# An MLP up projection by seven block products, and a down projection 512 columns at a time

## The chip, the cores and the metric

The kernel runs on one core of one Trainium2 chip. The metric is the device time of one execution in microseconds; a kernel's time is the median of its runs.

## What is computed

One layer of a bidirectional encoder, batch 1, 512 tokens, width 1024, f32. A modulation vector comes from c; then

```python
h = rmsnorm(x, norm_mix_w[l]) * (1.0 + scale1) + shift1
proj = h @ w_in[l]
y_ssd = ssd_mixer(z, xbc, dt_raw, ...)      # Mamba-2 SSD, 16 heads, both directions
y_hg = hgrn2_mixer(q, f_fwd, f_bwd, i, g, ...)  # HGRN2, 8 heads, both directions
y = jnp.concatenate([y_ssd, y_hg], axis=-1).astype(x.dtype) @ w_out[l]
x = x + gate1 * y
h = rmsnorm(x, norm_mlp_w[l]) * (1.0 + scale2) + shift2
x = x + gate2 * (jnp.square(jax.nn.relu(h @ w_up[l])) @ w_down[l])
```

and a last RMSNorm. `w_up` is 1024 x 4096, `w_down` 4096 x 1024. The MLP takes 512 tokens through both.

## The kernel before

All large products are made in three parts. An f32 operand is split into `hi`, its value rounded to the type fp32r that TensorE reads in one pass, and the residue `lo`; a product is hi·hi + hi·lo + lo·hi, three matmuls into one PSUM tile. The split of a piece of 128 x 512 weights is a cast on ScalarE (`hi`) and a subtraction on VectorE (`lo`). Raw weights come by DMA from SyncE's queue into four buffers (`raw`), split pieces lie in seven (`hi`, `lo`).

TensorE's instructions keep the order of the code. Those of the other engines are put in order by the compiler's scheduler, under the buffers and the data they wait for. In the mixing stage the code itself decides when a side stream (the SSD, the HGRN2 heads, the modulation sums) issues its next step: `Clock` adds up estimated costs, and `tick()` advances a stream that is due while the estimate of VectorE's and ScalarE's work is less than 3.5 us ahead of TensorE's.

PSUM has eight buffers of 128 x 512 in four rings: `mm` 2, `sc` 3, `tr` 2, `y` 1.

After the output projection (x in `x1`, tokens on partitions) the MLP begins. `h2_tile(tt)` turns the normalised rows of one tile of 128 tokens into columns: eight transposes, scale and shift out of PSUM (half on VectorE, half on ScalarE), then the split into `g_hi` and `g_lo`, whose partitions are the width and whose columns are the tokens. In the code tiles 0 and 1 stand within the output projection, tiles 2 and 3 among the first up products.

The MLP goes through four blocks of 1024 hidden columns. A block has four up units and four down units. An up unit takes 256 hidden columns: for each of two column tiles, eight row tiles of the width, three matmuls of 512 tokens each (`mm_T`); `relu2` takes the result out of PSUM (relu, square, split into `uh` and `ul`, two passes on each of ScalarE and VectorE). A down unit takes 256 output columns: for each of the four token tiles, eight hidden tiles, three matmuls of 256 columns (`mm_N`), and `gated_add` multiplies by the gate and adds to `x1`, both on VectorE. The pieces of the next unit are loaded and split while a unit runs. The first unit and a half run in halves of 256 tokens, so that they can begin before tiles 2 and 3 of h exist. In the last unit each token tile is normalised and stored as it ends.

In the SSD, `intra(q)` multiplies, for each of four heads, a 128 x 128 matrix `es` with 64 columns of `xs`, in f32, into the PSUM tile `py`. There are two groups, four chunks, eight heads in each.

Of the kernel before, what the change touches and what calls it, by code (L numbers as in the profile page):

```python
# [151 lines left out]
def encoder_layer(  # L152
# [1208 lines left out]
    first = unit_split(mload(units[0]))
    raw2 = mload(units[1])
    w = unit_split(raw2, range(3))
    os_ = [psum("mm"), psum("mm"), psum("sc")]
    for j in range(2):
        mm_T(first, j, g_hi, g_lo, pst=os_[j], n=256)
        h2_tile(2 + j)
    mm_T(w, 0, g_hi, g_lo, pst=os_[2], n=256, ks=range(6))
    for j in range(2):
        mm_T(first, j, g_hi, g_lo, pst=os_[j], n0=256, n=256)  # L1370
        relu2(units[0], j, os_[j])
    w += unit_split(raw2, range(3, 4))
    mm_T(w, 0, g_hi, g_lo, pst=os_[2], n=256, ks=range(6, 8))
    mm_T(w, 0, g_hi, g_lo, pst=os_[2], n0=256, n=256)
    units = units[1:]
    for i, u in enumerate(units):
        nw = []
        if i + 1 < len(units):
            nxt = mload(units[i + 1])
            nw = unit_split(nxt, range(3))  # L1380

        def last():
            if nw:
                nw.extend(unit_split(nxt, range(3, 4)))
        if u[0] == "up":
            for j in range(2):
                if j:
                    pend.append(last)
                relu2(u, j, os_[2] if i == j == 0 else mm_T(w, j, g_hi, g_lo, hook=tick))
        else:  # L1390
            while len(gate2) <= u[2] // 2:
                bga.advance()

            def lh(k, tt, fb_=u[1]):
                return us[fb_, k][0][:, tt * P:(tt + 1) * P]

            def ll(k, tt, fb_=u[1]):
                return us[fb_, k][1][:, tt * P:(tt + 1) * P]
            if u == units[-1]:
                fnw = mp.tile([P, D], F32, tag="fnw", name="fnw")  # L1400
                nc.scalar.dma_start(out=fnw, in_=final_norm_w.partition_broadcast(P))
                c = slice(768, 1024)
                for tt in range(NT):
                    row_head(tt, 768)
                    V.tensor_tensor(out=xn2[:, tt, :768], in0=x1[:, tt, :768], in1=fnw[:, :768], op=MULT)
                for tt in range(NT):
                    o = psum("mm")
                    mm_N(w, tt, lh, ll, o[:, :256], 256)
                    gated_add(o[:, :256], tt, 1, c, gate2)
                    row_rstd(tt, 768)  # L1410
                    r = rs2[:, tt:tt + 1]
                    n = 448 if tt == 3 else 768
                    A.activation(xn2[:, tt, :n], xn2[:, tt, :n], AF.Copy, scale=r)
                    V.scalar_tensor_tensor(out=xn2[:, tt, c], in0=x1[:, tt, c], scalar=r, in1=fnw[:, c], op0=MULT, op1=MULT)
                    if n < 768:
                        V.tensor_scalar(out=xn2[:, tt, n:768], in0=xn2[:, tt, n:768], scalar1=r, scalar2=None, op0=MULT)
                        nc.scalar.dma_start(out=out2d[tt * P:(tt + 1) * P, :n], in_=xn2[:, tt, :n])
                        nc.sync.dma_start(out=out2d[tt * P:(tt + 1) * P, n:], in_=xn2[:, tt, n:])
                    else:
                        nc.sync.dma_start(out=out2d[tt * P:(tt + 1) * P, :], in_=xn2[:, tt, :])  # L1420
                break
            if u[2] == 0:

                os_ = [psum("mm"), psum("mm"), psum("sc"), psum("sc")]
                for k0, k1 in ((0, 6), (6, 8)):
                    for tt in range(NT):
                        mm_N(w, tt, lh, ll, os_[tt][:, :256], 256, ks=range(k0, k1))
                    if k0 == 0:
                        last()
                for tt in range(NT):  # L1430
                    gated_add(os_[tt][:, :256], tt, 1, slice(0, 256), gate2)
            for pair in range(2 if u[2] else 0):
                o = psum("mm")
                for i2 in range(2):
                    if pair and i2:
                        pend.append(last)
                    mm_N(w, 2 * pair + i2, lh, ll, o[:, i2 * 256:(i2 + 1) * 256], 256, hook=tick)
                gated_add(o, 2 * pair, 2, slice(u[2] * 256, u[2] * 256 + 256), gate2)
        w = nw


# [32 lines left out]
```

## Time and profile before

| | us |
|---|---|
| median of three runs | 995.55 (994.33 to 995.98) |
| profiled execution, its own time | 997.37 |
| its span, first to last instruction | 995.6 |

The profile is one execution. TensorE (PE) is the busiest engine; PEld is its weight load, which overlaps matmuls; DVE is VectorE, ACT is ScalarE. Operations are recorded by helpers, so lines 106, 170 and 175 stand for nearly all of them: groups are told apart by the names of their tiles. `ps_mm<-hi,uh` is a matmul into `mm`. One f32 matmul (not fp32r) shows as two records.

### The profile page before, as it was taken

Reading aid. Unit: us, or ns where it says so; the run is one execution under the profiler, and the core shown is the slowest. Engines: PE = TensorE matmul, PEld = TensorE weight load, DVE = VectorE, ACT = ScalarE, POOL = GpSimd, SP = SyncE. Lnnn points to the kernel's source line nnn. Section 1 sums busy time; section 2 is a strip of 40 time slices with the busy share of each in tenths; the row PEclk is TensorE's granted clock in tenths of the full one; section 3 lists DMA queues with packets and bytes.
Section 4 is the critical chain, followed back from the end, with each engine's and each line's share of the span. In section 5 each row is a group of like instructions: output and inputs, shape, how many; then the busy total and the mean of one; then the engine's idle time right before and its main releaser. Section 6 shows DMA issues by size and latency. Waiting matters only on the chain.

```text
span 995.6 us, 17588 instructions
## 1 busy us (share of the span) xinstructions
PE 962.5 (97%) x6886; PEld 843.9 (85%) x6886; DVE 649.2 (65%) x1189; ACT 493.9 (50%) x965; POOL 48.1 (5%) x91
## 2 busy tenths in 40 slices
PE   5999999999999999989999999999999999999997
PEld 4788887788877888879998899979988998998897
DVE  4478869887989475877777677665544455444445
ACT  6367647857675366565555225642233234214414
POOL 0000000010000000000111211000000000000000
PEclk9999999999999989999999999999999999999999
DMA  9953422334422333222656875133332233223322
GB/s 272 266 134 82 111 76 64 86 96 127 109 81 77 97 106 84 66 75 65 191 168 191 283 244 147 58 114 100 98 114 85 86 105 106 88 85 96 105 66 85
DMA packets 114791, 116.70 MB, mean 117 GB/s; under 512 B 8556, under 2 KB 103445, under 8 KB 114709
## 3 DMA queue, kind: packets, MB, share of 16 engines
q1 hardware_dynamic: 106213, 86.45, 29.7%
q0 software_dynamic: 8064, 28.32, 9.2%
q8 instruction: 54, 0.88, 0.4%
q10 hardware_dynamic: 432, 0.82, 0.2%
q14 instruction: 28, 0.23, 0.1%
HBM read 113.39 MB, written 2.16 MB: 116 GB/s over the span
## 4 chain that ended last, share of the span: by engine, by line
PE 87%; DVE 4%; DMA 3%; ACT 3%; issue 2%; SPq 0%; DVEq 0%; ACTq 0%; POOLq 0%
PE ps_mm L170 65%; PE ps_sc L170 13%; PE ps_tr L170 4%; PE ps_y L170 3%; PE ps_tr L175 2%; DMA raw<-in_w_in_dram 1%; DMA e<-cdr 1%; DVE K L106 1%; ACT hi L106 1%; DMA adaw<-in_ada_w_dram 1%; ACT t L106 1%; DVE lo L106 0%; DVE ada L106 0%; DVE Q L106 0%; DVE t L106 0%
## 5 line engine op out<-in xcount | busy, mean ns | idle before, releaser
L106 ACT CAST hi<-raw 128x512 fp32r<-128x512 f32 (+1 forms) x276 | 167.1, 614 | 240.7 <-PE ps_mm L170 156.7
L106 DVE TENSOR_TENSOR lo<-raw,hi 128x512 fp32r<-128x512 f32 (+1 forms) x276 | 185.5, 681 | 108.4 <-ACT hi L106 106.2
L170 PE MATMUL ps_mm<-hi,uh 128*128 128x256 f32 x448 | 125.8, 281 | 0.0
L170 PE MATMUL ps_mm<-hi,ul 128*128 128x256 f32 x448 | 125.4, 280 | 0.0
L170 PE MATMUL ps_mm<-lo,uh 128*128 128x256 f32 x448 | 125.4, 280 | 0.0
L170 PE MATMUL ps_mm<-hi,h_hi 128*128 128x256 f32 (+1 forms) x384 | 114.3, 298 | 0.0
L170 PE MATMUL ps_mm<-h_hi,hi 128*128 128x512 f32 x256 | 107.9, 422 | 1.1 <-ACT h_hi L106 1.1
L170 PE MATMUL ps_mm<-lo,h_hi 128*128 128x256 f32 (+1 forms) x384 | 108.2, 282 | 0.0
L170 PE MATMUL ps_mm<-hi,h_lo 128*128 128x256 f32 (+1 forms) x384 | 108.1, 282 | 0.0
L170 PE MATMUL ps_mm<-h_hi,lo 128*128 128x512 f32 x256 | 101.7, 397 | 0.0
L170 PE MATMUL ps_mm<-h_lo,hi 128*128 128x512 f32 x256 | 101.5, 397 | 0.0
L170 PE MATMUL ps_mm<-m_hi,hi 128*128 128x512 f32 (+1 forms) x264 | 100.7, 381 | 0.7 <-ACT m_hi L106 0.7
L170 PE MATMUL ps_mm<-m_lo,hi 128*128 128x512 f32 (+1 forms) x264 | 100.7, 382 | 0.6 <-DVE m_lo L106 0.6
L170 PE MATMUL ps_mm<-m_hi,lo 128*128 128x512 f32 (+1 forms) x264 | 100.7, 382 | 0.0
L170 PEld LDWEIGHTS ps_mm<-hi,uh 128*128 128x128 f32 x448 | 84.3, 188 | 0.4 <-issue 0.2
L170 PEld LDWEIGHTS ps_mm<-lo,uh 128*128 128x128 f32 x448 | 84.2, 188 | 0.4 <-issue 0.2
L170 PEld LDWEIGHTS ps_mm<-hi,ul 128*128 128x128 f32 x448 | 84.4, 188 | 0.0
L106 ACT ACTIVATE t<-ps_mm 128x512 f32<-128x512 f32 x63 | 37.4, 594 | 76.8 <-PE ps_mm L170 76.2
L170 PEld LDWEIGHTS ps_mm<-hi,h_hi 128*128 128x128 f32 x384 | 72.4, 189 | 3.5 <-issue 1.7
L170 PEld LDWEIGHTS ps_mm<-lo,h_hi 128*128 128x128 f32 x384 | 72.5, 189 | 1.9 <-issue 1.7
L170 PEld LDWEIGHTS ps_mm<-hi,h_lo 128*128 128x128 f32 x384 | 72.4, 189 | 0.0
L106 DVE TENSOR_TENSOR t<-t 128x512 f32<-128x512 f32 x32 | 22.1, 692 | 64.9 <-ACT uh L106 64.9
(301 smaller groups left out, 1967.6 us busy)
## 6 DMA issues: line engine op xcount, KB each, us to landing
raw<-in_w_in_dram SPq DMA_DIRECT2D x68, 256.0 KB, 2.9
adaw<-in_ada_w_dram POOLq DMA_DIRECT2D x32, 512.0 KB, 5.1
raw<-in_w_up_dram SPq DMA_DIRECT2D x64, 256.0 KB, 3.0
raw<-in_w_down_dram SPq DMA_DIRECT2D x64, 256.0 KB, 3.1
raw<-in_w_in_dram SPq DMA_DIRECT2D x104, 128.0 KB, 2.8
ada_in<-in_ada_w_dram SPq DMA_DIRECT2D x16, 512.0 KB, 6.1
e<-cdr POOLq DMA_DIRECT2D x32, 256.0 KB, 3.6
raw<-in_w_out_dram SPq DMA_DIRECT2D x32, 256.0 KB, 5.1
```

The costliest lines, as they stand in the source:

```text
L106: return f(*args, **kw)
L170: return tc.keep_in_program_order(nc.tensor.matmul(**kw))
L175: return tc.keep_in_program_order(nc.tensor.transpose(**kw))
```

## The change

The up projection. The 1024 x 512 matrix of h (width by tokens) is cut into 2 x 2 blocks, A11 (width 0 to 511, tokens 0 to 255), A12 (width 512 to 1023), A21 and A22 (tokens 256 to 511), and a group of hidden columns of `w_up` likewise into B11, B12, B21, B22 (512 rows by 256 columns, the two column halves 512 apart). Instead of eight block products there are seven (Winograd's form), on sums of blocks:

| product | h | weights |
|---|---|---|
| P1 | A11 | B11 |
| P2 | A12 | B21 |
| Q3 | S4 = A12 - S2 | B22 |
| Q4 | A22 | last sum of weights |
| Q5 | S1 = A21 - A22 | B11 + B12 |
| Q6 | S2 = A11 - S1 | B11 + B12 + B22 |
| Q7 | S3 = A11 - A21 | B12 + B22 |

(the signs are folded into the combinations). `h_sums` makes the four sums of h once, on VectorE, and splits them. For each of the eight groups (four blocks, two groups each) `up_prep` makes four sums of weight blocks on VectorE, each 128 x 1024, and splits fourteen pieces; the first two groups take the pieces of P1 and P2 from the row loads. A product is 2 column tiles x 4 row tiles x 3 matmuls of 256 columns. Its result is combined with earlier ones by VectorE on the way out of PSUM; `relu2` then works on 1024 elements at once, with three passes on ScalarE and one on VectorE. `ahead()` keeps seven split pieces in front of the one in use.

The down projection. `dn_wide` takes 512 output columns, the hidden tile in the outer loop and four token tiles in four PSUM tiles. In the last block columns 512 to 1023 keep 256 columns at a time (`dn_narrow`).

The start. `h2_tile` leaves its rows in `xn2`, from which `h_sums` reads. P1 and P2 of both first groups run before the rest, around `h2_tile(2)` and `h2_tile(3)`.

The SSD. Each product of `intra` becomes two, of 64 output rows each.

```diff
             def intra(q):
                 for h in range(4):
                     c0_ = (4 * q + h) * 64
-                    PE.matmul(out=py[:, c0_:c0_ + 64], lhsT=es[cc, q][:, h, :], rhs=yv[:, c0_:c0_ + 64], start=True, stop=True)
+                    for t0 in (0, 64):
+                        PE.matmul(out=py[t0:t0 + 64, c0_:c0_ + 64], lhsT=es[cc, q][:, h, t0:t0 + 64], rhs=yv[:, c0_:c0_ + 64],
+                                  start=True, stop=True)
...
     def h2_tile(tt):
         for q in range(2):
             pt = psum("tr")
-            hraw = tmp()[:, :T]
+            hraw = xn2[:, tt, q * T:(q + 1) * T]
...
+            if q == 0 and tt >= 2:
+                continue
             hv = hraw.rearrange("p (j n) -> p j n", n=P)
...
+    def h_sums():
...
+        V.tensor_tensor(out=fold(s1), in0=A21, in1=A22, op=SUB)
+        V.tensor_tensor(out=fold(s2), in0=A11, in1=fold(s1), op=SUB)
+        V.tensor_tensor(out=fold(s3), in0=A11, in1=A21, op=SUB)
+        V.tensor_tensor(out=fold(s4), in0=A12, in1=fold(s2), op=SUB)
...
+        for name, v, hi, lo in zip(("S2", "S1", "S3", "S4"), (s2, s1, s3, s4), his, los):
+            A.copy(out=hi, in_=v)
+            V.tensor_tensor(out=lo, in0=v, in1=hi.bitcast(F32), op=SUB)
...
+    def up_load(g, b):
...
+        t = up_.tile([P, 4, 256], F32, tag="xr", name=nm("xr"), bufs=5)
+        r, c0_ = (b // 10 - 1) * 512, g // NS * 1024 + (b % 10 - 1) * 512 + g % NS * 256
+        nc.sync.dma_start(out=t, in_=w_up2[r:r + 512, c0_:c0_ + 256].rearrange("(k p) n -> p k n", p=P))
+        blocks_in[g, b] = t
+
+    def up_prep(g):
+        early = g < NS
...
+        if not early:
+            yield from halves(b11)
+        V.tensor_tensor(out=b11, in0=b11, in1=b12, op=ADD)
+        x2 = up_.tile([P, 4, 256], F32, tag="xr", name=nm("xr"), bufs=5)
+        V.tensor_tensor(out=x2, in0=b11, in1=b22, op=ADD)
+        yield from halves(x2)
+        yield from halves(b11)
+        up_load(g + 1, 11)
+        V.tensor_tensor(out=b12, in0=b12, in1=b22, op=ADD)
+        yield from halves(b12)
+        up_load(g + 1, 12)
+        if not early:
+            yield from halves(b21)
+        yield from halves(b22)
+        up_load(g + 1, 22)
+        V.tensor_tensor(out=x2, in0=x2, in1=b21, op=ADD)
+        yield from halves(x2)
+        up_load(g + 1, 21)
...
+    def up_step(g, what, tag):
+        o = psum(tag)
+        for i in range(2):
+            hi, lo = pieces[used[0]]
+            for k in range(4):
+                mh_, ml_ = mov[PRODUCTS[what]](k)
+                mm3(o[:, i * 256:(i + 1) * 256], hi[:, k, :], lo[:, k, :], mh_, ml_, k == 0, k == 3)
+            used[0] += 1
+            ahead()
...
+        if what == "Q6":
+            wt_[g] = tmp()[:, :T].rearrange("p (i n) -> p i n", n=256)
+            V.tensor_tensor(out=wt_[g], in0=o3, in1=p1s[g], op=SUB)
+        elif what == "Q5":
+            tt_[g] = tmp()[:, :T].rearrange("p (i n) -> p i n", n=256)
+            V.tensor_tensor(out=tt_[g], in0=o3, in1=wt_[g], op=ADD)
+        elif what == "Q7":
+            V.tensor_tensor(out=c22, in0=tt_[g], in1=o3, op=SUB)
+            V.tensor_tensor(out=c21, in0=o3, in1=wt_[g], op=SUB)
...
+    def relu2(g, half):
+        r = rt[g][half]
...
+        A.activation(r, r, AF.Relu)
+        A.activation(r, r, AF.Square)
+        A.copy(out=uh, in_=r)
         V.tensor_tensor(out=ul, in0=r, in1=uh.bitcast(F32), op=SUB)
...
+    def dn_wide(fb_, c, tags):
+
+        os_ = [psum(t) for t in tags]
+        for n_, k in enumerate(KDN):
+            hi, lo = pieces[used[0]]
+            for tt in range(NT):
+                uh, ul = u_at(fb_, k, tt)
+                PE.matmul(out=os_[tt], lhsT=uh, rhs=hi[:, 0, :], start=n_ == 0, stop=False)
+                PE.matmul(out=os_[tt], lhsT=uh, rhs=lo[:, 0, :], start=False, stop=False)
+                PE.matmul(out=os_[tt], lhsT=ul, rhs=hi[:, 0, :], start=False, stop=n_ == 7)
...
+        for tt in range(NT):
+            gated_add(os_[tt], tt, 1, slice(c * T, c * T + T), gate2)
...
+    for b in (11, 12, 22, 21):
+        up_load(0, b)
+    for _ in range(4):
+        wpump()
+    ahead()
+    up_step(0, "P1", "mm")
+    h2_tile(2)
+    up_step(1, "P1", "mm")
+    h2_tile(3)
+    h_sums()
+    for g in range(NS):
+        up_step(g, "P2", "sc")
+    for fb_ in range(NF):
+        for s_ in range(NS):
+            g = fb_ * NS + s_
+            if fb_:
+                up_step(g, "P1", "mm" if s_ else "sc")
+            up_step(g, "Q6", "y")
+            up_step(g, "Q5", "sc")
+            up_step(g, "Q7", "sc")
+            if fb_:
+                up_step(g, "P2", "mm")
+            up_step(g, "Q3", "sc")
+            up_step(g, "Q4", "sc")
+        dn_wide(fb_, 0, ("mm", "y", "sc", "sc"))
+        if fb_ < NF - 1:
+            dn_wide(fb_, 1, ("mm", "sc", "mm", "y"))
```

`wpump` issues the next 256 KB load of a raw piece. The end of the kernel (the last 256 columns, norm and store of each token tile) is as before, with its buffers in other memory.

## Rows read from the trace of the kernel before

**Rows 1.** The page, busy time: us, share of the span, instructions of each engine.
```profile
PE 962.5 (97%) x6886; PEld 843.9 (85%) x6886; DVE 649.2 (65%) x1189; ACT 493.9 (50%) x965; POOL 48.1 (5%) x91
```

**Rows 2.** Busy time by stretch: length, engines with their counts, PEclk, DMA share, GB/s.
```profile
200.00:300.00 100.00, 98.75 (x800) 83.80 (x799) 83.04 (x151) 67.23 (x138) 8.06 (x15) 1.00 0.38 104
...
574.00:603.00 29.00, 29.00 (x246) 28.91 (x246) 20.40 (x36) 9.23 (x17) 3.39 (x5) 1.00 0.74 240
603.00:640.00 37.00, 33.84 (x282) 33.03 (x282) 24.06 (x60) 20.66 (x50) 2.84 (x4) 1.00 0.28 83
696.20:785.80 89.60, 89.60 (x579) 81.26 (x578) 42.35 (x69) 28.28 (x47) 0.00 (x0) 1.00 0.30 94
```

**Rows 3.** Chain that ended last, from 590 us: start, length, engine, tile, instructions.
```profile
645.50 18.07 PE ps_mm L170 x78
...
678.41 4.25 PE ps_sc L170 x36
```

**Rows 4.** Timeline of VectorE, 785 to 800 us: start, length, operation, idle before.
```profile
787.78 0.68 DVE L106 TENSOR_TENSOR t<-ps_mm,hold 128x512 f32<-128x512 f32 x1
788.38 0.68 DVE L106 TENSOR_TENSOR lo<-raw,hi 128x512 fp32r<-128x512 f32 x1
788.98 0.69 DVE L106 TENSOR_TENSOR x<-x,t 128x512 f32<-128x512 f32 x1
```

**Rows 5.** Timeline of VectorE, 980 to 983 us.
```profile
981.06 0.95 DVE L106 TENSOR_TENSOR xn<-x,fnw 128x768 f32<-128x768 f32 x1
981.93 0.42 DVE L106 TENSOR_TENSOR t<-ps_mm,hold 128x256 f32<-128x256 f32 x1
```

**Rows 6.** Timeline of VectorE, 684 to 687 us.
```profile
683.96 0.75 DVE L106 TENSOR_TENSOR t<-ps_mm,hold 128x256 f32<-128x256 f32 x2
```

**Rows 7.** Groups of the whole span by shape, ScalarE: count, busy us, mean ns.
```profile
L106 ACT CAST hi<-raw 128x512 fp32r<-128x512 f32 x264 | 162.2, 620 | 238.7 <-PE ps_mm L170 156.7 <-PE ps_sc L170 46.0 <-DMA raw<-in_w_out_dram 12.1
...
L106 ACT ACTIVATE sqv<-xn 128x1024 f32<-128x1024 f32 x4 | 4.2, 1054 | 0.6 <-DMA xn<-in_x_dram 0.6
```

**Rows 8.** Timeline of VectorE, 623 to 642 us.
```profile
625.20 1.29 DVE L106 TENSOR_TENSOR m_lo<-t,m_hi 128x512 fp32r<-128x512 f32 x2 [0.69 <-ACT m_hi L106]
626.41 0.42 DVE L106 TENSOR_TENSOR t<-ps_mm,hold 128x256 f32<-128x256 f32 x1
...
628.39 0.49 DVE L106 TENSOR_SCALAR xn<-x,rs 128x512 f32<-128x512 f32 x1
...
633.59 1.37 DVE L106 TENSOR_SCALAR t<-ps_tr,a,b 128x128 f32<-128x128 f32 x4 [0.69 <-PE ps_tr L175]
```

**Rows 9.** Timeline of TensorE, 624.4 to 626.2 us.
```profile
625.22 0.39 PE L170 MATMUL ps_mm<-m_hi,hi 128*128 128x256 f32 x1 [0.71 <-ACT m_hi L106]
625.94 0.39 PE L170 MATMUL ps_mm<-m_lo,hi 128*128 128x256 f32 x1 [0.34 <-DVE m_lo L106]
```

**Rows 10.** Busy time by stretch of 5 us, columns as in rows 2.
```profile
360.00:365.00 5.00, 2.78 (x24) 2.59 (x23) 4.12 (x8) 3.59 (x9) 0.00 (x0) 1.00 0.16 42
365.00:370.00 5.00, 5.00 (x25) 4.93 (x25) 3.34 (x10) 1.92 (x5) 0.55 (x2) 0.53 0.70 206
```

**Rows 11.** DMA issues, 590 to 700 us: KB each, median us to landing.
```profile
adaw<-in_ada_w_dram POOLq DMA_DIRECT2D x7, 512.0 KB, 4.4
```

**Rows 12.** Timeline of TensorE, 342 to 344 us.
```profile
342.18 1.89 PE L170 MATMUL ps_y<-xs,e 128*128 128x64 f32 x16
343.91 0.65 PE L170 MATMUL ps_sc<-st,ct 128*128 128x512 f32 x1
```

**Rows 13.** Timeline of TensorE, 451.6 to 453.6 us.
```profile
451.62 0.69 PE L170 MATMUL ps_sc<-q,hy 128*64 128x64 f32 x16
...
453.36 0.39 PE L170 MATMUL ps_mm<-hi,h_hi 128*128 128x256 f32 x1
```

**Rows 14.** Weight loads by shape, 200 to 460 us: count, busy us, mean ns.
```profile
L170 PEld LDWEIGHTS ps_sc<-Q,hy 128*64 128x64 f32 x512 | 18.6, 138 | 6.5 <-issue 4.0 <-PE ps_mm L170 0.4 <-ACT hy L106 0.4
L170 PEld LDWEIGHTS ps_y<-xs,e 128*128 128x128 f32 x128 | 16.7, 209 | 0.4
```

More of the change, by code (lines that the diff above doesn't have):

```diff
@@ L1361, in encoder_layer @@
[L1361 to L1389, printed above, removed]
-        else:
[L1391 to L1439, printed above, removed]
@@ new lines, in encoder_layer, with wpump, row_tile, load @@
+    wq_in, wq_out = [], []
+    def wpump():
+        if wq_in:
+            wq_out.append(wq_in.pop(0)())
+    def row_tile(src, r, c0_, ncols, nk):
+        def load():
+            raw = wp.tile([P, 544], F32, tag="raw", name=nm("raw"), bufs=4)
+            v = raw[:, :nk * ncols].rearrange("p (k n) -> p k n", n=ncols)
+            nc.sync.dma_start(out=v, in_=src[r:r + nk * P, c0_:c0_ + ncols].rearrange("(k p) n -> p k n", p=P))
+            return v
+        return load
+    def parts_of(raw, nk, ncols):
+        hi = wp.tile([P, 544], F32R, tag="hi", name=nm("hi"))[:, :512].rearrange("p (k n) -> p k n", n=ncols)
+        lo = wp.tile([P, 544], F32R, tag="lo", name=nm("lo"))[:, :512].rearrange("p (k n) -> p k n", n=ncols)
+        A.copy(out=hi, in_=raw)
+        V.tensor_tensor(out=lo, in0=raw, in1=hi.bitcast(F32), op=SUB)
+        return hi, lo
@@ new lines, in encoder_layer, with halves @@
+    pieces, blocks_in = [], {}
+    def up_load(g, b):
+        if g >= NF * NS:
+            return
+        t = up_.tile([P, 4, 256], F32, tag="xr", name=nm("xr"), bufs=5)
[4 more added lines that the diff above has]
+        early = g < NS
+        def halves(t):
+            for i in range(2):
+                pieces.append(parts_of(t[:, :, i * P:(i + 1) * P], 4, P))
+                yield
+        b11, b12, b22, b21 = (blocks_in.pop((g, b)) for b in (11, 12, 22, 21))
+        if not early:
[16 more added lines that the diff above has]
+        up_load(g + 1, 21)
@@ new lines, in encoder_layer, with queue_prep, prep_all @@
+    KDN = (0, 1, 4, 5, 6, 7, 2, 3)
+    def queue_prep(n, nk, ncols):
+        for _ in range(n):
+            raw = wq_out.pop(0)
+            pieces.append(parts_of(raw, nk, ncols))
+            wpump()
+            yield
+    def prep_all():
+        yield from queue_prep(8, 4, P)
+        for fb_ in range(NF):
+            for s_ in range(NS):
+                yield from up_prep(fb_ * NS + s_)
+            yield from queue_prep(16 if fb_ < NF - 1 else 8, 1, 512)
+        yield from queue_prep(8, 2, 256)
@@ new lines, in encoder_layer, with ahead @@
+    for r in (0, 512):
+        for j in range(4):
+            wq_in.append(row_tile(w_up2, r, j * P, P, 4))
+    for fb_ in range(NF):
+        for c0_ in (0, 512) if fb_ < NF - 1 else (0,):
+            wq_in += [row_tile(w_down2, (fb_ * 8 + k) * P, c0_, 512, 1) for k in KDN]
+    for c0_ in (512, 768):
+        wq_in += [row_tile(w_down2, ((NF - 1) * 8 + KDN[q]) * P, c0_, 256, 2) for q in range(0, 8, 2)]
+    prep, made, used = prep_all(), [0], [0]
+    def ahead():
+        while made[0] < used[0] + 7 and next(prep, prep) is not prep:
+            made[0] += 1
@@ new lines, in encoder_layer @@
+    us, p1s, wt_, tt_, rt = {}, {}, {}, {}, {}
+    PRODUCTS = {"P1": "A11", "Q6": "S2", "Q5": "S1", "Q7": "S3", "P2": "A12", "Q3": "S4", "Q4": "A22"}
+    def up_step(g, what, tag):
+        o = psum(tag)
+        for i in range(2):
+            hi, lo = pieces[used[0]]
[4 more added lines that the diff above has]
+            ahead()
+        o3 = o.rearrange("p (i n) -> p i n", n=256)
+        if what == "P1":
+            p1s[g] = up_.tile([P, 2, 256], F32, tag="p1", name=nm("p1"), bufs=2)
+            A.copy(out=p1s[g], in_=o3)
+            return
+        if g not in rt:
+            rt[g] = [up_.tile([P, 2, T], F32, tag=f"r{i}", name=nm("r")) for i in range(2)]
+        c11, c21, c12, c22 = (rt[g][i][:, :, n:n + 256] for i in range(2) for n in (0, 256))
+        if what == "Q6":
[7 more added lines that the diff above has]
+            V.tensor_tensor(out=c21, in0=o3, in1=wt_[g], op=SUB)
+        elif what == "P2":
+            V.tensor_tensor(out=c11, in0=o3, in1=p1s[g], op=ADD)
+        elif what == "Q3":
+            V.tensor_tensor(out=c12, in0=o3, in1=tt_[g], op=ADD)
+            relu2(g, 1)
+        else:
+            V.tensor_tensor(out=c21, in0=o3, in1=c21, op=ADD)
+            relu2(g, 0)
+        tick()
@@ new lines, in relu2, with u_at @@
+    def relu2(g, half):
+        r = rt[g][half]
+        uh = up_.tile([P, 2, T], F32R, tag="uh", name=nm("uh"), bufs=4)
+        ul = up_.tile([P, 2, T], F32R, tag="ul", name=nm("ul"), bufs=4)
+        A.activation(r, r, AF.Relu)
+        A.activation(r, r, AF.Square)
+        A.copy(out=uh, in_=r)
+        V.tensor_tensor(out=ul, in0=r, in1=uh.bitcast(F32), op=SUB)
+        for i in range(2):
+            us[g // NS, half * 4 + g % NS * 2 + i] = (uh[:, i, :], ul[:, i, :])
+    def u_at(fb_, k, tt):
+        uh, ul = us[fb_, k]
+        return uh[:, tt * P:(tt + 1) * P], ul[:, tt * P:(tt + 1) * P]
@@ new lines, in dn_narrow @@
+    def dn_narrow(fb_, tt, o):
+        for n_, k in enumerate(KDN):
+            hi, lo = pieces[used[0] + n_ // 2]
+            uh, ul = u_at(fb_, k, tt)
+            PE.matmul(out=o, lhsT=uh, rhs=hi[:, n_ % 2, :], start=n_ == 0, stop=False)
+            PE.matmul(out=o, lhsT=uh, rhs=lo[:, n_ % 2, :], start=False, stop=False)
+            PE.matmul(out=o, lhsT=ul, rhs=hi[:, n_ % 2, :], start=False, stop=n_ == 7)
+    for b in (11, 12, 22, 21):
+        up_load(0, b)
+    for _ in range(4):
+        wpump()
@@ new lines, in encoder_layer @@
+    ahead()
+    up_step(0, "P1", "mm")
[5 more added lines that the diff above has]
+        up_step(g, "P2", "sc")
+    for fb_ in range(NF):
+        for s_ in range(NS):
+            g = fb_ * NS + s_
[11 more added lines that the diff above has]
+            dn_wide(fb_, 1, ("mm", "sc", "mm", "y"))
@@ new lines, in encoder_layer @@
+    fb_ = NF - 1
+    for pair in range(2):
+        o = psum("mm")
+        for i in range(2):
+            dn_narrow(fb_, 2 * pair + i, o[:, i * 256:(i + 1) * 256])
+        gated_add(o, 2 * pair, 2, slice(512, 768), gate2)
+    used[0] += 4
+    ahead()
+    fnw = up_.tile([P, 4, 256], F32, tag="xr", name="fnw", bufs=5).rearrange("p a n -> p (a n)")
+    nc.scalar.dma_start(out=fnw, in_=final_norm_w.partition_broadcast(P))
+    c = slice(768, 1024)
+    xn2 = ypool.tile([P, NT, D], F32, tag="hg_y", name="xn3")
@@ new lines, in encoder_layer @@
+    for tt in range(NT):
+        row_head(tt, 768)
+        V.tensor_tensor(out=xn2[:, tt, :768], in0=x1[:, tt, :768], in1=fnw[:, :768], op=MULT)
+    for tt in range(NT):
+        o = psum("mm")
+        dn_narrow(fb_, tt, o[:, :256])
+        gated_add(o[:, :256], tt, 1, c, gate2)
+        row_rstd(tt, 768)
+        r = rs2[:, tt:tt + 1]
+        n = 448 if tt == 3 else 768
+        A.activation(xn2[:, tt, :n], xn2[:, tt, :n], AF.Copy, scale=r)
+        V.scalar_tensor_tensor(out=xn2[:, tt, c], in0=x1[:, tt, c], scalar=r, in1=fnw[:, c], op0=MULT, op1=MULT)
+        if n < 768:
+            V.tensor_scalar(out=xn2[:, tt, n:768], in0=xn2[:, tt, n:768], scalar1=r, scalar2=None, op0=MULT)
+            nc.scalar.dma_start(out=out2d[tt * P:(tt + 1) * P, :n], in_=xn2[:, tt, :n])
+            nc.sync.dma_start(out=out2d[tt * P:(tt + 1) * P, n:], in_=xn2[:, tt, n:])
+        else:
+            nc.sync.dma_start(out=out2d[tt * P:(tt + 1) * P, :], in_=xn2[:, tt, :])
```

36 lines of the change are left out of this document (20 added, 16 removed).

## The prediction

> **What bounds the kernel now.** I read the page first, then the stretches, then single engines in the stretch that the change rewrites. The page shows TensorE busy for 97% of the span and VectorE for 65% [rows 1]. The stretches show where that matters: in a middle block of the MLP (from 696.2 us, 89.6 us long, three of them alike) TensorE has no idle time, its clock stands at 1.00, the 2.4 GHz level, while VectorE works 42 of 89.6 us and DMA is at 0.30 [rows 2]. So there a matmul taken away is time taken away, as long as VectorE and ScalarE keep up. At the MLP's start (603 to 640) TensorE lacks 3.2 us, and in the mixing stage (200 to 300) 1.3 us of 100: near its limit as well.
>
> **TensorE in the MLP.** The chain gives the pace of issue, which is shorter than the duration of one matmul because they overlap: 36 matmuls of 256 columns in 4.25 us are 0.118 us each, 78 of 512 columns in 18.07 us are 0.232 [rows 3]. A block checks it: 384 x 0.118 + 192 x 0.232 = 89.8 for 89.6 [rows 2]. I use 0.118 and 0.231. So a matmul of 512 columns costs nearly two of 256, and the count of columns is what sets the time, whatever the shape.
>
> Before: the up projection has 16 units of 48 matmuls of 512 columns, of which the first one and a half run as halves, so 696 of 512 and 144 of 256; the down projection has 16 x 96 of 256. After: 8 groups x 7 products x 2 column tiles x 4 row blocks x 3 parts = 1344 of 256 in the up projection; 7 wide passes x 96 = 672 of 512 and 192 of 256 in the down projection. The difference is 144 of 256 and 24 of 512: 144 x 0.118 + 24 x 0.231 = 22.5 us less. The two shapes and both kinds of operand stand in the trace, so this term has no bounds worth naming (0.5). A middle block falls from 89.6 to 336 x 0.118 + 192 x 0.231 = 84.0.
>
> **VectorE in a middle block.** An operation on 512 elements lasts 0.69, but back to back they start every 0.60 [rows 4]. For 1024 elements no row exists for two tensors; 768 elements let the next start after 0.87 [rows 5], so 0.27 more per 256 gives 1.13 (1.22 isolated). Per block after: 28 + 16 residues `lo` of 512, 8 block sums of 1024, 14 combinations out of PSUM, 4 residues `ul` of 1024, 16 operations of the gated sum: 74 x 0.60 + 12 x 1.13 = 58 us, against 84 of TensorE: 69%. The tight part is the up stage, 39.6 us of TensorE. Seven split pieces and three block sums are made in the stage before (seven buffers), so it needs 21 residues, 5 sums, 13 combinations, 2 `ul`, and the 8 gated operations left by the down stage: 42 x 0.60 + 7 x 1.13 = 33.1. It fits with 6 us to spare if the operations stand in a good order. The order is not that of the code: the code writes two pairs of product and sum, and the trace shows both products first [rows 6], and a residue slid in between a product and its sum [rows 4]. ScalarE has 44 casts of 0.62, two copies and 12 passes of 1024 elements at 1.05 [rows 7], 41 us of 84.
>
> Each later block can lose a little where the single PSUM buffer `y` is late: the last wide pass ends in it, and Q6 wants it one product (24 x 0.118 = 2.8 us) later, while VectorE has four products and up to three sums to do, begun 2.1 us earlier: between nothing and, if they all start behind one late residue, 1.4 + 7 x 0.69 - 2.8 = 3.5 us. I take 0.5 for each of three, 1.5, as the gated operations are seen to be reordered [rows 6].
>
> **The start of the MLP.** Now VectorE finishes the first two row tiles of h at 626.5 and is loosely used after that [rows 8]; TensorE begins the up projection at 625.2, waits for the residue until 625.9 [rows 9], and then goes through. After the change much more stands between 626.5 and the end of the first up stage: what row tile 3 of x has left (1.3), evictions and residues of two h tiles (2 x (1.37 + 0.60) = 3.9), four sums of h and their four residues (8 x 1.13 = 9.0), eight block sums (9.0), 28 pieces less the seven made ahead (21 x 0.60 = 12.6), 14 combinations (8.4), two `ul` (2.3): 46.5 us, so 673.0 without a gap. TensorE would need from 625.9 on 39.6 + 1.7 of transposes: 667.2. The last combinations (1.2) come behind the last matmul and the last piece comes 1.4 before it, so TensorE ends this stage near 673, 6 late. Gapless is a bound from below, less what is ready too early to count (4); with isolated durations the same list is 51.3 us (11). I take 7. The wait is paid at Q6, whose moving operand S2 comes from a chain: last h tile at 635.0, two sums, a cast and a residue of 1024 elements, 640 or later, where the eight products before it end at 639.
>
> A stall may cost the clock as well. Behind a stretch with 2.78 of 5 us busy the granted clock was 0.53, the 1.2 GHz level, for the next 5 us [rows 10]; that would be 2.4 us. But TensorE waits for VectorE here anyway, so I add nothing and leave it to the range.
>
> **The loads.** The same weights come in, 2 MB twice, and DMA has room [rows 2]. The first blocks land in memory that the output projection's weights held until 624.5 [rows 9]; 512 KB took 4.4 us to land [rows 11], and the first block sum is wanted after about 629: hidden. The first eight pieces are loaded through the old buffers, as now.
>
> **The intra products of the SSD.** One chunk's 8 fp32 products, 16 records, take 1.73 us (342.18 to 343.91) [rows 12]. Split into halves of 64 output rows they become 32 records of the form that the HGRN2 scores have: 48 of those (three rows of 16, the first shown, up to the next matmul) take 1.74 us, 0.036 each [rows 13], so 1.16. Eight chunks: 8 x 0.57 = 4.6 us less at most, nothing at least, if others set the time there. TensorE is nearly full in that stage, so I take 3.
>
> The Trainium skill, TensorEngine Tiling (Array Packing), "Restrictions", says that column tiling turns the fast weight load off, which speaks against this split. The rows say otherwise for fp32: a load of 64 columns took 138 ns, one of 128 columns 209 [rows 14]. If each half cost what a whole one costs now, the split would add 8 x 1.73 = 13.8 us; that is the fourth rival.
>
> **Sum.** The profiled execution took 997.4, its span 995.6. 997.4 - 22.5 + 7 + 1.5 - 3 = 980.4. The median of the runs is 1.8 below that execution: 978.5. A difference of 0.2%, 2 us, is about what can be told from no change.
>
> **Rivals.**
> First, the start costs nothing (VectorE does the sums in the gaps before 626.5 or the scores come cheap) and the split gives all its 4.6: 997.4 - 22.5 - 4.6 - 1.8 and some 2 for the rest, 971. For it: VectorE has 13 of 37 us free between 603 and 640 [rows 2]; against it, S2 needs the last h tile.
>
> Second, slower: VectorE's queue stays near the code's order. Then `ul` blocks it while ScalarE makes three passes of 1.05, and the up stage needs 21 x 0.69 + 5 x 1.22 + 13 x 0.69 + 2 x 1.22 + 8 x 0.69 + three such waits of 3.2 = 47 instead of 39.6: 7.6 a block, and 10 more in the first: 978.5 + 33 = 1011. It decides from 45 us per up stage on, where a block is no shorter than now. Against it speaks the order that the trace shows [rows 4, 6].
>
> Third, the load queue of SP keeps the code's order, in which the four block loads stand ahead of the first four piece loads. These then wait until 624.5, behind 2 MB, at the 240 GB/s seen in 574 to 603 [rows 2] 8.7 us, and a load (4.4 for twice its size [rows 11]) and a split more: the first product starts some 10 us late, with the h tiles behind it on TensorE: 988. Nothing in the trace tells, since SP's loads now all go through one ring of buffers.
>
> Fourth, the halves cost like whole ones: 978.5 + 3 + 13.8 = 995, no change.
>
> **Numbers.** Forecast 0.60 (974 to 984), first rival 0.14, second 0.09, third 0.12, fourth 0.05. Faster 0.60 + 0.14 + 0.12 = 0.86, same 0.05, slower 0.09. The range reaches from a little below the first rival to above the third: 968 to 992; outside are the second, the fourth and tails.
>
> **What would show it.** A middle block of 84 to 85 us with TensorE full and VectorE near 58; the 256-column pace still 0.118 where S sums and `lo` pieces meet; at the start a wait of several us before the first product into `y`, released by VectorE, and VectorE without gaps until about 673; 32 records of an SSD chunk in 1.2 us. I am wrong if the middle blocks show waits of TensorE on VectorE in each up stage, if the first w_up pieces land after 624, or if the clock falls in the MLP.

## The result and the profile after

The changed kernel took 978.85 us (median of four runs, 977.99 to 979.96) against 995.69 for the kernel before: ratio 0.9834, 95% interval 0.9817 to 0.9851. The forecast was 978.5. Its span in the profile is 976.1 us, 19.5 less than before; 2.2 of that lie in the first 53 us, where both programs issue the same matmuls and only the place of a stretch at 1.2 GHz differs, so the medians (16.8 less) are the better measure.

The page and the stretches of the changed kernel, to be laid beside [rows 1, 2]; columns as there:

```profile
PE 938.2 (96%) x6846; PEld 818.2 (84%) x6846; DVE 727.8 (75%) x1267; ACT 535.0 (55%) x1007; POOL 47.9 (5%) x91
```

```profile
200.00:300.00 100.00, 98.37 (x837) 82.03 (x837) 84.19 (x155) 69.03 (x142) 7.71 (x15) 1.00 0.36 101
...
616.10:633.90 17.80, 13.69 (x112) 13.28 (x112) 16.45 (x28) 11.59 (x24) 0.00 (x0) 0.95 0.45 143
633.90:641.30 7.40, 5.65 (x24) 5.36 (x25) 7.40 (x10) 4.17 (x6) 0.00 (x0) 0.50 0.12 41
641.30:667.70 26.40, 26.40 (x218) 26.23 (x218) 25.40 (x37) 14.33 (x22) 0.00 (x0) 0.98 0.51 157
712.20:796.90 84.70, 84.53 (x530) 76.07 (x529) 60.82 (x86) 38.75 (x58) 0.00 (x0) 1.00 0.33 100
```

The last row is a middle block: 84.7 us where [rows 2] had 89.6, TensorE full at clock 1.00, VectorE at 60.8. Three rows make the first up stage: VectorE works 16.45 + 7.40 + 25.40 = 49.25 of 51.6 us there, and TensorE lacks time only in the first two. In the middle one its clock is 0.50, the 1.2 GHz level. TensorE's timeline shows where that begins:

```profile
629.86 0.28 PE L170 MATMUL ps_sc<-m_hi,lo 128*128 128x256 f32 x1
633.90 0.58 PE L170 MATMUL ps_y<-m_hi,hi 128*128 128x256 f32 x1 [3.76 <-ACT m_hi L106]
636.23 0.58 PE L170 MATMUL ps_y<-m_lo,hi 128*128 128x256 f32 x1 [1.74 <-DVE m_lo L106]
636.61 0.42 PE L170 MATMUL ps_y<-m_hi,lo 128*128 128x256 f32 x1
636.83 0.41 PE L170 MATMUL ps_y<-m_hi,hi 128*128 128x256 f32 x1
```

Q6 is the product into `y`. It begins 4.0 us behind its forerunner, loses another 2.3 until the residue of S2 is there, and then goes on at 0.21 a matmul instead of 0.118. VectorE meanwhile:

```profile
627.12 1.04 DVE L106 TENSOR_SCALAR xn<-ps_tr,a,b 128x128 f32<-128x128 f32 x3
628.08 1.22 DVE L106 TENSOR_TENSOR s<-xn 128x1024 f32<-128x1024 f32 x1
629.21 0.69 DVE L106 TENSOR_TENSOR m_lo<-xn,m_hi 128x512 fp32r<-128x512 f32 x1
629.81 1.22 DVE L106 TENSOR_TENSOR s<-xn 128x1024 f32<-128x1024 f32 x1
630.95 0.69 DVE L106 TENSOR_TENSOR lo<-xr,hi 128x512 fp32r<-128x512 f32 x1
631.55 1.22 DVE L106 TENSOR_TENSOR s<-xn,s 128x1024 f32<-128x1024 f32 x1
632.68 1.22 DVE L106 TENSOR_TENSOR xr<-xr,xr 128x1024 f32<-128x1024 f32 x1
633.82 1.22 DVE L106 TENSOR_TENSOR s<-xn,s 128x1024 f32<-128x1024 f32 x1
634.95 1.22 DVE L106 TENSOR_TENSOR m_lo<-s,m_hi 128x1024 fp32r<-128x1024 f32 x1
```

No gap: evictions of the last h tile, the four sums `s` (the third is S2), a block sum `xr`, and only then S2's residue `m_lo`. Operations of 1024 elements start every 1.13, as estimated.

One SSD chunk (the 16 records of [rows 12], now 32 halves), and a later Q6:

```profile
337.37 1.15 PE L170 MATMUL ps_y<-xs,e 128*64 128x64 f32 x32
338.45 1.13 PE L170 MATMUL ps_sc<-st,ct 128*128 128x512 f32 x2
...
718.05 0.36 PE L170 MATMUL ps_y<-m_hi,hi 128*128 128x256 f32 x1 [0.17 <-DVE t L106]
```

1.08 us where it was 1.73; and the wait for `y` in a later block is 0.17. SyncE's queue put the w_up rows first and the blocks later, so no piece was late:

```profile
580.25 12.34 SPq L1389 DMA_DIRECT2D raw<-in_w_up_dram  x8
...
614.72 2.03 SPq L1408 DMA_DIRECT2D xr<-in_w_up_dram  x4
```

### The profile page after: what moved, and what is told of

It reads as the page before. It is cut to its first block, busy times and chain, and to the rows that moved or that the text cites. A ratio compares the mean times of both kernels' runs of the same rounds, so it can differ in the third digit from the quotient of the medians.

```text
span 976.1 us, 17630 instructions
## 1 busy us (share of the span) xinstructions
PE 938.2 (96%) x6846; PEld 818.2 (84%) x6846; DVE 727.8 (75%) x1267; ACT 535.0 (55%) x1007; POOL 47.9 (5%) x91
## 4 chain that ended last, share of the span: by engine, by line
PE 83%; DVE 7%; DMA 4%; ACT 3%; issue 2%; SPq 1%; DVEq 0%; ACTq 0%; POOLq 0%
PE ps_mm L170 43%; PE ps_sc L170 25%; PE ps_y L170 9%; PE ps_tr L170 4%; PE ps_tr L175 2%; DVE lo L106 1%; DVE t L106 1%; DMA e<-cdr 1%; DMA raw<-in_w_out_dram 1%; ACT hi L106 1%; DVE x L106 1%; DMA raw<-in_w_up_dram 1%; DVE ada L106 1%; DVE xn L106 1%; DVE m_lo L106 1%
## 5 line engine op out<-in xcount | busy, mean ns | idle before, releaser
L106 ACT CAST hi<-xr 128x512 fp32r<-128x512 f32 x104 | 61.4, 619 | 92.4 <-PE ps_y L170 41.6
L106 DVE TENSOR_TENSOR lo<-xr,hi 128x512 fp32r<-128x512 f32 x104 | 69.1, 686 | 21.3 <-ACT hi L106 20.9
L170 PEld LDWEIGHTS ps_mm<-h_hi,hi 128*128 128x128 f32 x256 | 48.3, 189 | 15.7 <-issue 3.5
L170 PE MATMUL ps_sc<-sl,hi 128*128 128x256 f32 x256 | 59.2, 283 | 0.0
L170 PEld LDWEIGHTS ps_mm<-h_lo,hi 128*128 128x128 f32 x256 | 48.2, 188 | 11.6 <-issue 1.4
L170 PEld LDWEIGHTS ps_mm<-h_hi,lo 128*128 128x128 f32 x256 | 48.1, 188 | 10.8
L106 DVE SCALAR_TENSOR_TENSOR ada<-adaw,cact,ada 128x512 f32<-128x512 f32 x56 | 41.9, 749 | 15.7 <-DMA adaw<-in_ada_w_dram 15.0
L170 PE MATMUL ps_mm<-hi,uh 128*128 128x512 f32 (+1 forms) x144 | 50.3, 350 | 0.9 <-DVE t L106 0.9
L106 DVE TENSOR_TENSOR Q<-Q,T 128x512 f32<-128x512 f32 x56 | 42.0, 750 | 11.4 <-PE ps_sc L170 11.3
L170 PE MATMUL ps_mm<-hi,ul 128*128 128x512 f32 (+1 forms) x144 | 49.4, 343 | 0.0
L170 PE MATMUL ps_mm<-lo,uh 128*128 128x512 f32 (+1 forms) x144 | 49.2, 342 | 0.0
```

Source lines behind the costliest of these rows:

```text
L106: return f(*args, **kw)
L170: return tc.keep_in_program_order(nc.tensor.matmul(**kw))
```

## The experiments

The start of the MLP moves by a few us from run to run with the clock stretches ahead of it. So beside each median stands the MLP's own length in the profile, from the start of the first matmul of the up projection to that of the last matmul of the kernel (two rows of TensorE's timeline), and the first up stage, to the first matmul of the down projection.

| kernel | median us | ratio to before, 95% | MLP | first up stage |
|---|---|---|---|---|
| before | 995.7 to 996.5 | | 363.4 | 48.8 |
| changed | 978.85 | 0.9817 to 0.9851 | 353.0 | 51.6 |
| 1 split alone | 989.5 | 0.991 to 0.9953 | 363.4 | 48.8 |
| 2 MLP alone | 985.38 | 0.9867 to 0.9921 | 353.0 | 51.6 |
| 3 eight products | 989.16 | 0.9895 to 0.9948 | 362.9 | 50.8 |
| 4 code order | 1011.09 | 1.0105 to 1.017 | 383.7 | 51.7 |
| 5 no sums | 975.89 | 0.9778 to 0.9841 | 351.7 | 49.3 |
| 6 S2 first | 979.67 | 0.9809 to 0.9867 | 353.0 | 51.6 |
| 7 P1 of four groups | 981.13 | 0.9824 to 0.9889 | 352.5 | 54.1 |
| 8 GpSimd | 982.0 | 0.9837 to 0.9892 | 356.5 | 55.0 |
| 9 short chain | 979.35 | 0.9817 to 0.9852 | 355.1 | 53.7 |
| 10 both | 976.53 | 0.9766 to 0.982 | 350.4 | 50.0 |
| 11 first group plain | 973.55 | 0.9735 to 0.9782 | 346.1 | 45.7 |

**1 and 2: the two halves of the change alone.** The split of `intra` put into the kernel before, and the changed kernel without it.

> The kernel before with the split of the SSD's intra products alone. If TensorE sets the time there and a half costs what the HGRN2 scores cost, each of eight chunks is 0.57 us shorter: 3 to 4.6 us less than before, about 992, with 32 records of a chunk in about 1.2 us. If the whole lead of 9.1 us that the changed kernel has at the MLP's start comes from this split, about 987. If each half costs like a whole one, 14 us more, about 1010.

> The changed kernel with the SSD's intra products whole again. If the MLP's share is what its part of the two traces shows (363.7 to 353.3 us from its first to its last matmul), about 10 to 12 us less than before, 984 to 986, and this and the split alone add up to the whole change. If the forecast's own terms held, 14 less, about 982. If the MLP gains only because the mixing stage ends in another state (clock, queues), under 5 less.

The split alone gave 6.7 us, between the 992 and the 987 of its expectation; the MLP alone gave 10.8, within its 984 to 986; together 17.4, for 16.8 of the whole. The MLP lengths say that the two don't touch each other: 363.4 and 353.0 are those of before and of the whole. The eight chunks (from the first half to the matmul behind the last) took 15.7 us before and 10.0 with the split: 5.7 of TensorE's time, more than the 4.6 that was held to be the most. One of them ran at the 1.2 GHz level in both (3.31 before, 1.91 after), which is 1.4 of the 5.7. The others took 1.73 to 1.83 before, and [rows 12] is one of the shorter; with the split all but one of them (1.73) took 1.03 to 1.08.

**3: how much comes from the seven products.** Eight products, 512 tokens at a time, with the wide down projection and the split kept.

```diff
-    def up_step(g, what, tag):
+    def up_unit(fb_, j):
+        os_ = [psum("mm"), psum("sc")]
...
+            for k in (2 * q, 2 * q + 1):
+                for i in range(2):
...
+                    mm3(os_[i], hi[:, k % 2, s], lo[:, k % 2, s], g_hi[:, k, :], g_lo[:, k, :], k == 0, k == 7)
```

> The changed kernel with the up projection as eight block products again (512 tokens at a time, no sums of h or of weights), the wide down projection kept, and the split of the SSD's products kept. By count the wide passes alone take 1344 matmuls of 256 columns to 672 of 512, 3.4 us less; with the split's 4 to 5 us about 987 to 989, and a block of 44.4 + 44.4 = 88.8 us. If the wide down projection had the larger part of the MLP's gain, 980 to 983; if it costs more than it saves, because four PSUM tiles are freed late, 992 or more.

989.16 is at the upper end of what the count gave and no different from the split alone (989.5), and the MLP is 0.5 shorter than before. Its later blocks are 0.7 shorter each, and its first up stage 2.0 longer, where TensorE waits 1.8 for a tile of h, as less work stands ahead of it. So the seven products are what shortens the MLP: 362.9 to 353.0.

**4: the order on VectorE.** In the two middle blocks VectorE keeps the order of the code; nothing else is changed.

```diff
+        V.pin = tc.keep_in_program_order if fb_ in (1, 2) else None
```

> The changed kernel with VectorE's instructions held to the order of the code in the second and third of the four blocks. The forecast's second rival says that an up stage then takes 7 to 8 us longer, because a residue of the activations stands before the split of the next pieces and waits for three passes of ScalarE: the two blocks go from 84.7 to about 92 us each, 993 to 996 in all. If VectorE has so much room (61 of 85 us) that the order is of no account, 979, blocks of 85.

Some 32 us slower than the changed kernel, and slower than the kernel before. TensorE's waits, over the whole span (total, times, longest):

```profile
PE ps_sc L171 <- DVE lo L106: 10.2, 4, 4.9
PE ps_y L171 <- DVE t L106: 8.6, 5, 4.4
```

VectorE and ScalarE ahead of one of the waits of 4.9:

```profile
747.10 0.68 DVE L106 TENSOR_TENSOR r<-ps_sc,r 128x512 f32<-128x512 f32 x1
751.93 1.23 DVE L106 TENSOR_TENSOR ul<-r,uh 128x1024 fp32r<-128x1024 f32 x1 [4.14 <-ACT uh L106]
753.08 2.49 DVE L106 TENSOR_TENSOR lo<-xr,hi 128x512 fp32r<-128x512 f32 x4
```

```profile
747.93 1.05 ACT L106 ACTIVATE r<-r 128x1024 f32<-128x1024 f32 x1
748.89 0.60 ACT L106 CAST hi<-xr 128x512 fp32r<-128x512 f32 x1
749.40 1.05 ACT L106 ACTIVATE r<-r 128x1024 f32<-128x1024 f32 x1
750.35 0.60 ACT L106 CAST hi<-xr 128x512 fp32r<-128x512 f32 x1
750.86 1.04 ACT L106 CAST uh<-r 128x1024 fp32r<-128x1024 f32 x1
```

`ul` holds VectorE for 4.1 us while ScalarE makes its three passes with casts between them, and four residues `lo` queue behind it, the first of which TensorE needs. Then the clock falls:

```profile
752.70:759.50 6.80, 5.69 (x26) 5.69 (x27) 6.06 (x10) 1.51 (x3) 0.00 (x0) 0.50 0.47 131
```

This is the second rival's mechanism, at twice its price: from down stage to down stage the three intervals are 30.5 us longer in all than those of the changed kernel, 15 for each of two blocks, not 7.6. Of the 30.5, 19.8 are more idle time of TensorE, and 9.0 are 92 matmuls at the 1.2 GHz level, which the rival had not priced. The order is what keeps the later blocks at 84.7.

**5 and 6: why is the first up stage late?** Theory A: the amount of VectorE's work. Theory B: the chain from the last h tile over S1 and S2 to Q6. Kernel 5 takes the eight block sums of the first two groups out (their products read unsummed blocks, so the MLP's values aren't the reference's); kernel 6 leaves all work and puts S2's split straight behind its sum.

```diff
-        V.tensor_tensor(out=b11, in0=b11, in1=b12, op=ADD)
+        if not early:
+            V.tensor_tensor(out=b11, in0=b11, in1=b12, op=ADD)
...
```

```diff
+        A.copy(out=g_hi[:, :4, 256:], in_=s2)
+        V.tensor_tensor(out=g_lo[:, :4, 256:], in0=s2, in1=g_hi[:, :4, 256:].bitcast(F32), op=SUB)
         V.tensor_tensor(out=fold(s3), in0=A11, in1=A21, op=SUB)
...
-        while made[0] < used[0] + 7 and next(prep, prep) is not prep:
+        while made[0] < min(used[0] + 7, cap_[0]) and next(prep, prep) is not prep:
```

> The changed kernel without the eight block sums of w_up in its first two groups: the products there take unsummed blocks, so the MLP's values of these groups are not the reference's. Nothing else is left out. That takes 8 x 1.13 = 9.0 us of work from VectorE in the first up stage, and not from TensorE. Theory A (VectorE bounds the first up stage; it is busy for 49 of 51.6 us there): the stage becomes 7 to 9 us shorter, and the half clock behind the wait at Q6 goes or shrinks, 968 to 972. Theory B (only the chain h tile, S1, S2, its split, then Q6 makes it late, with VectorE otherwise free enough): the sums that stand ahead of S2 in VectorE's queue are few, so 3.4 to 5.6 us are gained, 973 to 976.

> The changed kernel with another order of the same work at the start: S2 is split directly behind its sum, and no pieces beyond the first nine are split before the four sums of h are done. Nothing is left out. Theory A (VectorE's amount of work bounds the first up stage): the wait at Q6 shrinks but comes back in the products behind it; the stage's end moves by at most 2.3 us, 977 to 979. Theory B (the chain up to S2 makes it late): the wait of 6.2 us goes and with it the half clock, 971 to 973.

Without the sums the first up stage is 2.3 us shorter, not 7 to 9, and the MLP 1.3 (the median is 3.0 lower, but its interval overlaps that of the changed kernel). So Theory A misses here; 975.89 lies in Theory B's 973 to 976. With S2 first the stage doesn't move and the wait comes back behind Q6, which is what Theory A had, and Theory B's 971 to 973 misses. TensorE's waits in kernel 5, and then in kernel 6:

```profile
630.71 0.58 PE L170 MATMUL ps_y<-m_hi,hi 128*128 128x256 f32 x1 [2.81 <-ACT m_hi L106]
632.51 0.58 PE L170 MATMUL ps_y<-m_lo,hi 128*128 128x256 f32 x1 [1.22 <-DVE m_lo L106]
```

```profile
633.58 0.58 PE L170 MATMUL ps_y<-m_hi,hi 128*128 128x256 f32 x1 [2.56 <-ACT m_hi L106]
635.37 0.58 PE L170 MATMUL ps_y<-m_lo,hi 128*128 128x256 f32 x1 [1.21 <-DVE m_lo L106]
...
648.29 0.36 PE L170 MATMUL ps_sc<-s4h,hi 128*128 128x256 f32 x1 [2.28 <-DVE t L106]
```

With 9 us of work gone, the chain still makes Q6 wait 2.8 and 1.2, and the clock still falls behind it (0.50 from 630.6 to 637.2). With a shorter chain and all the work, Q6 waits as little, the clock falls too (0.50 from 633.0 to 639.8), and Q3 then waits 2.3 for VectorE's combination. So there are two limits close to each other: less work leaves the chain's wait, and a shorter chain, which was not taken away altogether, leaves the work's.

**7 and 8: more cover, or less work for VectorE.** P1 of four groups ahead instead of two; and the sums S3, S4 and their residues on GpSimd.

```diff
+    for g in (2, 3):
+        up_step(g, "P1", "mm")
...
-            if fb_:
+            if fb_ > 1:
                 up_step(g, "P1", "mm" if s_ else "sc")
```

```diff
-        V.tensor_tensor(out=fold(s3), in0=A11, in1=A21, op=SUB)
-        V.tensor_tensor(out=fold(s4), in0=A12, in1=fold(s2), op=SUB)
+        G.tensor_tensor(out=fold(s3), in0=A11, in1=A21, op=SUB)
+        G.tensor_tensor(out=fold(s4), in0=A12, in1=fold(s2), op=SUB)
...
-            V.tensor_tensor(out=lo, in0=v, in1=hi.bitcast(F32), op=SUB)
+            (G if name in ("S3", "S4") else V).tensor_tensor(out=lo, in0=v, in1=hi.bitcast(F32), op=SUB)
```

> The changed kernel with P1 of four groups instead of two run ahead, behind the h tiles: TensorE gets 2 x 24 x 0.118 = 5.7 us of work in place of the wait at Q6, taken from the second block; VectorE gets 4 residues more there (2.4 us) and 2 copies out of PSUM. Theory A (VectorE bounds the stage): of the 5.7 us some 2.5 to 3.5 are kept, as VectorE ends later by its additional work: 975 to 977; the clock may stay at full, 2 more. Theory B (the chain to S2): nearly all 5.7 and the clock are gained, 971 to 973.

> The changed kernel with the sums S3 and S4 and the residues of S3 and S4 on GpSimd instead of VectorE: 4 operations of 1024 elements, 4.5 us less on VectorE in the first up stage, nothing left out. Theory A (VectorE bounds the stage): 3 to 4.5 us less, 975, as long as GpSimd, which the trace shows idle there, makes each in less than some 4 us; with GpSimd at over 5 us for each, Q3 and Q7 wait for it and the time is 979 or more. Theory B (the chain to S2): S3 and S4 are not part of that chain, gain of 1 us or none, 978 to 979.

Both miss. In kernel 7 the stage without its added 5.7 us is 48.4, so 3.2 are gained, but P1 was the cover of `y` in the second block, and there Q6 now waits:

```profile
725.34 0.36 PE L170 MATMUL ps_y<-m_hi,hi 128*128 128x256 f32 x1 [2.86 <-DVE t L106]
```

In all the MLP is 0.5 shorter. That the median is 2.3 above the changed kernel's is not clear of noise, as the intervals overlap; in the profile the MLP begins later (621.0 for its first matmul, not 616.1), behind two stretches at clock 0.50 that the changed kernel's doesn't have (362.1 to 365.5 and 614.7 to 618.1). Kernel 8 has GpSimd and VectorE in each other's way, GpSimd's rows first:

```profile
626.13 2.40 POOL L1366 TENSOR_TENSOR s<-xn 128x1024 f32<-128x1024 f32 x1 [15.91 <-ACT xn L106]
632.09 3.19 POOL L1367 TENSOR_TENSOR s<-xn,s 128x1024 f32<-128x1024 f32 x1 [3.56 <-DVE s L106]
636.44 3.52 POOL L1374 TENSOR_TENSOR sl<-s,sl 128x1024 fp32r<-128x1024 f32 x1 [1.16 <-ACT sl L106]
```

```profile
626.75 2.33 DVE L106 TENSOR_TENSOR lo<-xr,hi 128x512 fp32r<-128x512 f32 x1
...
635.32 1.23 DVE L106 TENSOR_TENSOR sl<-s,s1h 128x1024 fp32r<-128x1024 f32 x1 [2.24 <-POOL s L1367]
636.46 1.22 DVE L106 TENSOR_TENSOR m_lo<-s,m_hi 128x1024 fp32r<-128x1024 f32 x1
...
638.20 6.36 DVE L106 TENSOR_TENSOR lo<-xr,hi 128x512 fp32r<-128x512 f32 x4
```

An `lo` of 0.69 takes 2.33 while GpSimd works, four of them 6.36 instead of 2.49 (the first two 2.31 and 2.92), and VectorE stands 2.24 behind a GpSimd sum. Not every operation suffers: the `m_lo` beside GpSimd's third row took its usual 1.22. The 4.5 us taken from VectorE cost more than they save: the MLP is 3.5 longer.

**9 to 11: both limits.** Kernel 9 is kernel 6 with row tile 3 of h transposed ahead of the second P1; kernel 10 is that without the sums (again not the reference's values); kernel 11 makes the first of the eight groups by plain products on unsummed blocks, with the split of S2 behind them, all work done.

```diff
     h2_tile(2)
-    up_step(1, "P1", "mm")
     h2_tile(3)
     h_sums()
+    up_step(1, "P1", "mm")
...
```

```diff
+    def plain(o, b, t, i):
+        n = slice(t * 256, t * 256 + 256)
+        for kb in range(2):
+            hi, lo = pieces[4 * b + 2 * i + kb]
+            for k in range(4):
+                mm3(o[:, i * 256:(i + 1) * 256], hi[:, k, :], lo[:, k, :], g_hi[:, 4 * kb + k, n], g_lo[:, 4 * kb + k, n],
+                    kb == 0 and k == 0, kb == 1 and k == 3)
...
+    plain(o00, 0, 0, 0)
     h2_tile(2)
-    up_step(1, "P1", "mm")
+    plain(o00, 0, 0, 1)
     h2_tile(3)
-    h_sums()
-    for g in range(NS):
-        up_step(g, "P2", "sc")
+    s2 = h_sums()
...
+    up_step(1, "P1", "mm")
+    up_step(1, "P2", "sc")
```

> The changed kernel with the chain up to Q6 shortened and no work removed: row tile 3 of h is transposed directly behind tile 2, ahead of P1 of the second group (24 products, 2.8 us), S2 is split directly behind its sum, and no more than nine pieces are split before the sums of h are done. Theory A+B (two limits close to each other: the amount of VectorE's work and the chain; taking away one leaves the other): the wait at Q6 falls to 2 us or less and comes back in Q3 or later, 976 to 979. Theory B alone (the chain): the wait goes and nothing comes back, 971 to 973.

> The kernel of the short chain, and without the eight block sums of w_up in the first two groups (their products take unsummed blocks, so the MLP's values are not the reference's). Without the sums alone 3.0 us were gained. Theory A+B (two limits): both are moved here, so 7 to 9 us are gained, 970 to 972. If the sums' 9 us were simply not in the way: as without the sums alone, 975 to 976.

> The changed kernel with the first group of hidden columns (of eight) by plain products on unsummed blocks, 192 matmuls of 256 columns instead of 168; nothing left out. TensorE gets 24 x 0.118 = 2.8 us more; VectorE loses four block sums, six residues and seven combinations of the first up stage (12 us), and S2 is wanted only some 28 us behind the first product. Theory A+B (the start is late by VectorE's amount and by the chain): the stage takes 44.5 to 46 instead of 50.9 and the clock stays at full, 972 to 974.5. If the start is late for another cause (the loads, ScalarE, the order on VectorE): 978 or more, as the added 2.8 us are not paid for.

Kernel 9 (979.35) came out just above what two limits gave, 976 to 979, for a mixed reason. Q6 waits 0.4 and 1.4, and Q3 2.6, but the transposes moved forward wait themselves, as tile 3 isn't normalised yet:

```profile
623.34 0.90 PE L175 MATMUL ps_tr<-cm,xn 128*128 128x128 f32 x5 [2.02 <-ACT xn L106]
...
648.81 0.36 PE L170 MATMUL ps_sc<-s4h,hi 128*128 128x256 f32 x1 [2.56 <-DVE t L106]
```

Kernel 10 has the same wait of 2.02 at 624.3 and missed its 970 to 972. Beside kernel 9, though, it shows the sums' worth with the short chain: 4.7 us of the MLP (355.1 to 350.4), where they were worth 1.3 with the long one (353.0 to 351.7). That speaks for two limits. Kernel 11 moves both at once and came out as they had it: 973.55, within 972 to 974.5, where another cause was to give 978 or more. Its first up stage:

```profile
618.60:664.40 45.80, 45.15 (x377) 44.75 (x378) 40.47 (x59) 31.14 (x54) 0.00 (x0) 1.00 0.47 146
```

TensorE is full, the clock stays at 1.00 and VectorE has 5 us left; 5.9 us less than 51.6, though TensorE does 2.8 us more. This is the fastest version: its interval (0.9735 to 0.9782) lies below that of the change (0.9817 to 0.9851).

## Why the forecast held, step by step

The sum was right by luck, as two errors cancel: the MLP gave 10.4 us in the profiles (10.8 alone), not the 14.0 of its three terms, and the split 5.7 to 6.7, not 3. What the MLP lacks is mostly the pace (1.3) and the start (2.6).

**The count, -22.5: right.** The trace has 1536 matmuls of 256 columns and 672 of 512 besides four of the modulation, as worked out. The middle blocks are 84.7, at the top of 84 to 85: a 256-column matmul of the up stages took 0.119 (48 in 5.70 us), not 0.118, which is 1.3 us over all 1344.

**The start, +7: place and releaser right, too small.** The stage ended 9.6 us behind what TensorE needs (50.9 from the second matmul at 616.84, against 41.3); 6.1 of it are the wait before Q6, released by VectorE, with VectorE nearly without gaps, as forecast (the "eight products" ahead of Q6 are four, of two column tiles each). The step that failed is "TensorE waits for VectorE here anyway, so I add nothing" for the clock: behind Q6's wait the 1.2 GHz level, which lasted until 642.3, slowed 28 matmuls of Q6 and Q5 to 0.21, 2.8 us in all, and from 641.3 on TensorE has no idle time (the stretch of 26.40 above), so nothing hid them. The last 0.7 of the 9.6 stay open. That the list of VectorE's work (46.5 us) sets the stage's end was half of the cause: kernel 5 shows that the chain to S2 makes most of the lateness even with 9 us of that list gone, kernel 6 that the work does with a shorter chain, and kernel 11 that the lateness goes when S2 is wanted later and VectorE has less to do. How large each would be alone stays open, as kernels 9 and 10 met another wait.

**The later blocks, +1.5: about right in sum, not in place.** Q6's wait for `y` is 0.15 to 0.17 in each of three, where 0.5 was taken; 0.85 is lost once, between the two passes of the first down stage. That is 1.3 in all.

**The split, -3: mis-sized.** Most chunks take 1.03 to 1.08, not 1.16, and all of it shortens the kernel, as far as the noise lets one tell: 5.7 over eight chunks, 6.7 in the medians, where 3 were taken in the belief that other engines would set part of the time. The fourth rival is refuted. The Trainium skill, TensorEngine Tiling (Array Packing), "Restrictions", has column tiling turn the fast weight load off; no run here shows a loss. The Trainium skill, TensorE: Matmul & The Clock Gate, "Weight-path perf modes", says that this load is on only for operands that aren't FP32, so that an fp32 product has none to lose. The 209 and 138 ns of [rows 14] agree with it.

**The rivals.** A free start with the whole 4.6 (971): no, the start cost 9.6. VectorE near the code's order (1011): not what happened, but kernel 4, which forces it, took 1011.09. The agreement is chance: two blocks at 15, where the rival had 7.6 in each of three and 10 more in the first. SyncE's queue in code order: no, the w_up rows were issued from 580.25.

## What to carry to other kernels

A scheme with fewer products and more sums is paid on the engine that makes the sums, and it is paid where the pipeline starts: count that engine's work in the first stage alone, and the chain to the first operand that exists only as a sum of sums. Start such a scheme with a plain group: here it cost TensorE 2.8 us more of matmuls, and the stage was still 5.9 shorter, as the wait and the low clock were gone. An order of the second engine found by the scheduler can be worth more than the change itself (here 30.5 us over two blocks, against 16.8), so look at it before believing in a busy share.
